# A hybrid encoder layer on one core: three of the seven staged SwiGLU combinations are split before they go to DRAM

## The chip, the cores and the metric

The kernel runs on one core of one Trainium2 chip, as one launch. The metric is the device time in microseconds, lower is better. The core has a matrix engine (TensorE, in the profile PE for its matmuls and PEld for its weight loads), a vector engine (VectorE, DVE), a scalar engine (ScalarE, ACT), GpSimd (POOL) and a queue engine that issues the DMAs (SyncE, SP). Matmuls accumulate in PSUM banks of 128 x 512 f32; all else lies in SBUF or in DRAM.

## The reference

One layer over 1024 tokens of width 1024: a SwiGLU half step, a combined mixer (HGRN2 heads and stick-breaking attention heads), a cross attention to 256 memory tokens, a second SwiGLU half step and a final norm. The change touches only the two SwiGLUs:

```python
D_FF = 2816

def swiglu(h, w_gu, w_down):
    gu = h @ w_gu
    gate, up = jnp.split(gu, 2, axis=-1)
    return (jax.nn.silu(gate) * up) @ w_down

x = x + 0.5 * swiglu(rmsnorm(x, ffn1_norm[l]), ffn1_w_gu[l], ffn1_w_down[l])
...
x = x + 0.5 * swiglu(rmsnorm(x, ffn2_norm[l]), ffn2_w_gu[l], ffn2_w_down[l])
```

The products are to have f32 accuracy. The kernel gets it by writing each factor as a high part (rounded to the matrix engine's fp32r) and a low part (the factor minus its high part), and by three matmuls for each pair of factors: high x high, high x low, low x high. Making a factor's two parts is called its split below: ACT copies the factor to the high part, DVE subtracts the high part from it.

## The kernel before

**Blocks and products.** All large products of a SwiGLU are done as jobs on 2 x 2 blocks in Winograd's form, with seven block products in place of eight. PRODUCTS (line 245) lists them: left factors A11, S1, S2, A12, S3, S4, A22 (weights or sums of weights), right factors B11, T1, T2, B21, T3, B22, T4 (activations or combinations of them), and the bank X, Y or Z that each adds to. One product is 12 matmuls of 128 x 512 (four row chunks of three matmuls each).

**Jobs.** The 2816 hidden columns are 22 chunks of 128, taken as 11 pairs p = 0 to 10. For each pair there is a gate job (gate_job) and an up job (up_job); pair 0 is done plainly ahead of the woven part. After the gate and the up job of a pair, four tiles a11, a12, a21, a22 of 128 x 512 hold its activations. store (line 792) forms from them T1 = a12 - a11, T2 = a22 - T1, T3 = a22 - a12, T4 = a21 - T2 with DVE, and SP writes seven tiles, B11 = a11, B21 = a21, B22 = a22 and T1 to T4, to DRAM (256 KB each). The second projection is made of down jobs (down_job, line 864): GROUPS (line 636) gathers the pairs as 0 to 3, 4 to 7 and 8 to 10, and each group has four down jobs, one for each quarter of the output columns. They are called group 0, 1 and 2 below. In the second SwiGLU the last group holds only pairs 8 and 9 (plain_last); pair 10 is multiplied plainly at the very end and stores only four tiles, a12 under the name T3. A product of group 2 thus has 9 matmuls in the first SwiGLU and 6 in the second.

**The return.** When group g starts, its seven combinations are fetched for its three or four pairs: fetches (line 822) loads each combination's tiles into the place of the low part (staged, line 806), seven products ahead of their first use; four products ahead ACT copies the high parts, three products ahead DVE subtracts in place. The split parts then serve all four jobs of the group. Names in the profile: T is a tile with both parts of a T1, T2 or T4; hh and hl are the high and the low part of B11, B21, B22 and T3; f is a split weight block, S a sum of weight blocks (made by POOL), r the raw weights, E and e are 128 x 512 activation or output tiles, sg a small pool of four such tiles, fa0B to fa10B and fa0T to fa10T (ga... in the second SwiGLU) the DRAM tiles.

**The order of the work.** Two streams of jobs (gate jobs and then down jobs with e = 0, 2; up jobs and then down jobs with e = 1, 3) are woven product by product, the second lagging by 3 products (weave, line 314; LAG, line 247). Each engine's recorded instructions keep the order in which the program emits them (in_order, line 71), so all of them carry line 83 in the profile. At each product i, weave.run issues the product's matmuls, the read of its bank (which frees the bank for the next product), the deferred steps that have come due (defer(n, step) runs a step n products later), and then prepares the products ahead by fixed leads (line 248):

```python
LOAD, SUM, FETCH, HI, LO, FETCHED_HI, FETCHED_LO = 7, 6, 7, 5, 4, 4, 3
```

So DVE's queue holds, in the order of the products: bank reads, low parts of weight blocks, the gating products, the combinations of store, and at a group's start the low parts of the fetched tiles, three or four at a time. There are two PSUM buffers for each of X, Y and Z. In group 1 of a SwiGLU the residual x, which has been put away in DRAM, is brought back through tiles of the sg pool (to_x, line 814). Pair 0's tiles are stored by a deferred step (line 984).

Of the kernel before, what the change touches and what calls it, by code (L numbers as in the profile page):

```python
# [8 lines left out]
F32 = mybir.dt.float32  # L9
# [9 lines left out]
P = 128  # L19
# [12 lines left out]
def hybrid_layer(ctx, tc, x, mem, ffn1_norm, ffn1_w_gu, ffn1_w_down, mix_norm, w_in, hg_lb_raw,  # L32
# [611 lines left out]
        return hp.tile([P, H], F32R, name=f"hh{c}_{hf}"), hp.tile([P, H], F32R, name=f"hl{c}_{hf}")  # L644

    NORMED = 8

    def swiglu(rs, ys, g0, w_gu, w_down, blk, first, tag, done, tail, head, stored=False, hook=None, side=None, plain_last=False, lift=None):
        with ExitStack() as st:
# [1 line left out]
            psx = pool(st, "psx", 1, PSUM, "right")  # L651
            B = {"B11": [hT[0][2 * j] for j in range(4)], "B21": [hT[0][2 * j + 1] for j in range(4)],
                 "B22": [hT[1][2 * j + 1] for j in range(4)], "T1": [], "T2": [], "T3": [], "T4": []}
            ad = [{k: dram.tile([P, H], F32, name=f"{tag}a{p}{k}") for k in B} for p in range(FP)]
            xd = {}
            pools = {}

            def E(brief=False):
                if brief or "ep" not in pools:
                    return pools["e0"].tile([P, H], F32, name="e")  # L660
                return pools["ep"].tile([P, H], F32, name="E")
# [115 lines left out]
            def up_job(p):  # L777
# [11 lines left out]

                return job(blk, w_gu, 0, 4, FF + 2 * p * P, B.get, summed(u[p], use))  # L790

            def store(p, a11, a12, a21, a22):
                if plain_last and p == FP - 1:
                    for k, t in (("B11", a11), ("B21", a21), ("B22", a22), ("T3", a12)):
                        nc.sync.dma_start(out=ad[p][k], in_=t)
                    return
                t1, t2, t3, t4 = (E(i < 2) for i in range(4))
                dve.tensor_tensor(t1, a12, a11, op=ALU.subtract)
                dve.tensor_tensor(t2, a22, t1, op=ALU.subtract)
                dve.tensor_tensor(t3, a22, a12, op=ALU.subtract)  # L800
                dve.tensor_tensor(t4, a21, t2, op=ALU.subtract)
                for k, t in (("B11", a11), ("T1", t1), ("B22", a22), ("T2", t2), ("T3", t3), ("B21", a21), ("T4", t4)):
                    nc.sync.dma_start(out=ad[p][k], in_=t)


            def staged(p, bk, n):
                hi, lo = slot(blk, bk, n)
                nc.sync.dma_start(out=lo.bitcast(F32), in_=ad[p][bk])
                return hi, lo

            acc = {}
# [10 lines left out]
            def fetches(p0, pn):  # L822
                Bg = {}

                def fetch(bk, what):
                    if what == 0 and bk not in Bg:
                        Bg[bk] = [staged(p0 + n, bk, n) for n in range(pn)]
                        stack[p0, bk] = 0
                    if what and stack[p0, bk] < what:
                        stack[p0, bk] = what  # L830
                        for hi, lo in Bg[bk]:
                            if what == 1:
                                act.activation(hi, lo.bitcast(F32), AF.Copy)
                            else:
                                dve.tensor_tensor(lo, lo.bitcast(F32), hi.bitcast(F32), op=ALU.subtract)

                return Bg.get, fetch
# [26 lines left out]
            def down_job(p0, pn, e, get, fetch):  # L864
                ends = (p0, pn) == last_group[0]

                def read(fk, bank):
# [6 lines left out]
                    if plain_last and ends:  # L874
                        if (e, fk) == (1, "A11"):
                            for half, ks in enumerate((("B11", "B21"), ("T3", "B22"))):
                                plains[half] = [staged(FP - 1, k, 3) for k in ks]
                            for n, t in enumerate(plains[0] + plains[1]):
                                pairs.defer(7 + n, lambda t=t: split_staged([t]))
                            pairs.defer(1, load_rows_last)  # L880
                        elif (e, fk) == (2, "A22"):
                            for n, (k, b) in enumerate(((0, 0), (0, 1), (1, 0), (1, 1))):
# [98 lines left out]
            pairs.defer(1, lambda: flow([sums_4(2), sums_4(3)], 2))  # L981
            pairs.defer(2, x_away)
            pairs.defer(4, open_mp)
            pairs.defer(14, lambda: store(0, s[0][0], s[1][0], s[0][1], s[1][1]))
            pairs.run()

            if plain_last:
# [719 lines left out]
```

## Time and profile before

| | |
|---|---|
| median of 3 runs | 2322.42 us (2320.59 to 2324.09) |
| the profiled execution | 2320.99 us |
| its span, from the first to the last instruction | 2319.3 us |
| mean granted clock of TensorE | 0.991 |
| bytes moved by DMA | 228.03 MB (HBM read 166.49, written 59.51) |

The gate and up jobs of the first SwiGLU lie between about 86 and 442 us of the span, those of the second between about 1705 and 2055 us; the down jobs follow each. The profile's page gives for each engine its busy time, its share of the span and its count of instructions. The view of windows gives the same for a stretch of time, with the granted clock of TensorE, the share in which the DMA engines were busy, and the GB/s they moved. The view of waits lists who was waited for: the waiting engine and its line, an arrow, the engine, tile and line that released it, then the total in us, the number of times and the longest. In a timeline a row is a start, a duration, the engine, the operation with output, inputs, shape and count, and in brackets the idle time of the engine before it and what ended that. Matmuls overlap: one lasts 0.39 us in such a row, though the next starts after 0.23 us.

### The profile page before, as it was taken

How to read it: one execution, taken by the hardware profiler on the slowest of the kernel's cores; microseconds unless marked ns; L12 is line 12 of the kernel's file. 1: busy time of each engine (PE TensorE's matmuls, PEld its weight loads, DVE VectorE, ACT ScalarE, POOL GpSimd, SP SyncE). 2: the span in 40 equal slices, each digit the busy share in tenths (PEclk: the TensorE clock that was granted, in tenths of full speed). 3: DMA queues.
4: the chain of work that ended last, by engine and by line, in shares of the span. 5: the costliest groups of instructions: out<-in, count | busy, mean ns of one | idle time of the engine just before them, and what ended most of it. 6: DMA issues, size and time to landing. Idle time of an engine off the chain costs nothing. (4 is left out here: it accounts for less than half of the span.)

```text
span 2319.3 us, 31224 instructions
## 1 busy us (share of the span) xinstructions
PE 2236.2 (96%) x11330; PEld 1869.4 (81%) x11330; DVE 1692.2 (73%) x2832; ACT 980.0 (42%) x1885; POOL 731.5 (32%) x686
## 2 busy tenths in 40 slices
PE   8899999999999999999999999999989999999988
PEld 7788888777778788888979888887778888878767
DVE  5866667869985878778697536567586666786997
ACT  6434333444354536344364333224443333344334
POOL 2343446434541102011032020001335343643543
PEclk9999999999999999999999999999999999999999
DMA  6243333545622000001005311111332323274441
GB/s 218 90 138 109 123 109 118 196 135 160 192 93 64 19 29 28 28 28 28 27 25 169 118 37 55 46 37 41 123 132 91 117 94 111 90 236 130 135 135 73
DMA packets 198665, 228.03 MB, mean 98 GB/s; under 512 B 10928, under 2 KB 140016, under 8 KB 198512
## 3 DMA queue, kind: packets, MB, share of 16 engines
q1 hardware_dynamic: 198512, 226.04, 30.2%
q8 instruction: 89, 1.46, 0.3%
q14 instruction: 64, 0.52, 0.1%
HBM read 166.49 MB, written 59.51 MB: 97 GB/s over the span
## 5 line engine op out<-in xcount | busy, mean ns | idle before, releaser
L83 PE MATMUL X<-T,f 128*128 128x512 f32 x1464 | 348.0, 393 | 14.7 <-ACT e L83 10.8
L83 PEld LDWEIGHTS X<-T,f 128*128 128x128 f32 x1464 | 276.7, 190 | 75.2 <-ACT e L83 11.7
L83 PE MATMUL X<-hh,f 128*128 128x512 f32 x975 | 316.1, 394 | 15.6 <-DVE E L83 14.1
L83 ACT ACTIVATE f<-S 128x512 fp32r<-128x512 f32 (+2 forms) x256 | 154.4, 608 | 347.0 <-POOL S L83 346.6
L83 DVE TENSOR_TENSOR f<-S,f 128x512 fp32r<-128x512 f32 (+2 forms) x256 | 255.3, 1005 | 27.4 <-ACT f L83 25.9
L83 PEld LDWEIGHTS X<-hh,f 128*128 128x128 f32 x975 | 185.2, 190 | 59.6 <-ACT f L83 9.2
L83 POOL TENSOR_TENSOR E<-E,rs 128x512 f32<-128x512 f32 x112 | 180.0, 1608 | 121.5 <-DVE E L83 104.3
L83 DVE TENSOR_TENSOR f<-r,f 128x512 fp32r<-128x512 f32 (+2 forms) x192 | 200.8, 1063 | 0.3
L83 POOL TENSOR_TENSOR S<-r,r 128x512 f32<-128x512 f32 (+2 forms) x64 | 97.0, 1515 | 316.1 <-DVE E L83 93.6
L83 PE MATMUL X<-hl,f 128*128 128x512 f32 x488 | 192.4, 394 | 2.8 <-DVE hl L83 2.8
L83 PE MATMUL Y<-T,f 128*128 128x512 f32 x732 | 177.0, 390 | 0.2 <-DVE T L83 0.2
L83 PEld LDWEIGHTS Y<-T,f 128*128 128x128 f32 x732 | 137.2, 188 | 29.6 <-DVE T L83 1.1
L83 PE MATMUL Z<-hh,f 128*128 128x512 f32 x488 | 160.7, 389 | 0.0
L83 PE MATMUL Y<-hh,f 128*128 128x512 f32 x488 | 160.7, 389 | 0.0
L137 PE MATMUL acc<-hh,wh 128*128 128x512 f32 (+1 forms) x384 | 153.1, 399 | 0.0
L83 POOL TENSOR_TENSOR S<-S,r 128x512 f32<-128x512 f32 (+2 forms) x64 | 82.3, 1286 | 211.6 <-DVE f L83 211.6
L138 PE MATMUL acc<-hl,wh 128*128 128x512 f32 (+1 forms) x384 | 145.1, 378 | 1.4 <-DMA hl<-msl 1.4
L139 PE MATMUL acc<-hh,wl 128*128 128x512 f32 (+1 forms) x384 | 145.3, 378 | 0.0
L83 ACT ACTIVATE E<-X 128x512 f32<-128x512 f32 x102 | 60.5, 594 | 192.8 <-PE X L83 192.8
L1140 POOL TENSOR_SCALAR_AFFINE_SELECT om<-om 128x128 f32<-128x128 f32 x64 | 27.2, 424 | 355.2 <-ACT om L1135 354.9
L83 DVE TENSOR_TENSOR E<-X,E 128x512 f32<-128x512 f32 x98 | 67.3, 686 | 84.3 <-PE X L83 84.1
L117 ACT ACTIVATE wh<-wraw 128x512 fp32r<-128x512 f32 (+1 forms) x128 | 79.0, 654 | 103.1 <-PE acc L138 41.6
(465 smaller groups left out, 5490.4 us busy)
## 6 DMA issues: line engine op xcount, KB each, us to landing
r<-in_ffn_w_gu_dram SPq DMA_DIRECT2D x86, 512.0 KB
r<-in_ffn_w_down_dram SPq DMA_DIRECT2D x32, 512.0 KB
wraw<-in_w_in_dram SPq DMA_DIRECT2D x20, 512.0 KB
wraw<-in_mem_w_kv_dram SPq DMA_DIRECT2D x16, 512.0 KB
T<-in_x_dram SPq DMA_DIRECT2D x8, 512.0 KB
fx<-x SPq DMA_DIRECT2D x16, 256.0 KB
sg<-fx SPq DMA_DIRECT2D x16, 256.0 KB
xs<-E SPq DMA_DIRECT2D x16, 256.0 KB
```

Source lines behind the costliest of these rows:

```text
L83: done = getattr(self.eng, name)(*args, **kw)
L117: nc.scalar.activation(hi[:, part], src[:, part], AF.Copy)
L137: nc.tensor.matmul(ps, lh, rh, start=start, stop=False)
L138: nc.tensor.matmul(ps, lh, rl, start=False, stop=False)
L139: last_mm[0] = nc.tensor.matmul(ps, ll, rh, start=False, stop=stop).ins
L1140: nc.gpsimd.affine_select(out=a[:, dg], in_=a[:, dg], compare_op=ALU.is_gt, fill=fill, base=0, pattern=[[-1, P]], channel_multiplier=1)
```

## The change

SPLIT names three combinations, T1, B21 and T4. When a pair is stored, these three are split first: ACT copies the high part into a tile of the sg pool (for pair 0 into one of the pools of e or E tiles) and SP stores it; one product later DVE subtracts the high part in place, and SP stores the low part. On return both parts are loaded, each by a DMA of its own, and the copy and the subtraction at lead 4 and 3 are left out for them. T2, B11, T3 and B22 are stored whole and split on return as before. Beside this, the seven tiles of a pair are stored in another order, pair 0 is stored one product earlier, and in the second SwiGLU the four tiles of pair 10 are stored one to four products after their turn, one at a time.

```diff
--- before.py
+++ after.py
@@ -644,6 +644,7 @@
         return hp.tile([P, H], F32R, name=f"hh{c}_{hf}"), hp.tile([P, H], F32R, name=f"hl{c}_{hf}")
 
     NORMED = 8
+    SPLIT = ("T1", "B21", "T4", )
 
     def swiglu(rs, ys, g0, w_gu, w_down, blk, first, tag, done, tail, head, stored=False, hook=None, side=None, plain_last=False, lift=None):
         with ExitStack() as st:
@@ -651,7 +652,7 @@
             psx = pool(st, "psx", 1, PSUM, "right")
             B = {"B11": [hT[0][2 * j] for j in range(4)], "B21": [hT[0][2 * j + 1] for j in range(4)],
                  "B22": [hT[1][2 * j + 1] for j in range(4)], "T1": [], "T2": [], "T3": [], "T4": []}
-            ad = [{k: dram.tile([P, H], F32, name=f"{tag}a{p}{k}") for k in B} for p in range(FP)]
+            ad = [{k: [dram.tile([P, H], F32, name=f"{tag}a{p}{k}{e}") for e in ("hl" if k in SPLIT else "a")] for k in B} for p in range(FP)]
             xd = {}
             pools = {}
 
@@ -789,23 +790,39 @@
 
                 return job(blk, w_gu, 0, 4, FF + 2 * p * P, B.get, summed(u[p], use))
 
+            def keep(p, k, t):
+
+                if k not in SPLIT:
+                    nc.sync.dma_start(out=ad[p][k][0], in_=t)
+                    return
+                hi = pools["sg"].tile([P, H], F32, name="sg") if p else E()
+                act.activation(hi.bitcast(F32R), t, AF.Copy)
+                nc.sync.dma_start(out=ad[p][k][0], in_=hi)
+
+                def low():
+                    dve.tensor_tensor(t.bitcast(F32R), t, hi, op=ALU.subtract)
+                    nc.sync.dma_start(out=ad[p][k][1], in_=t)
+
+                pairs.defer(1, low)
+
             def store(p, a11, a12, a21, a22):
                 if plain_last and p == FP - 1:
-                    for k, t in (("B11", a11), ("B21", a21), ("B22", a22), ("T3", a12)):
-                        nc.sync.dma_start(out=ad[p][k], in_=t)
+                    for n, (k, t) in enumerate((("B11", a11), ("B21", a21), ("B22", a22), ("T3", a12))):
+                        pairs.defer(1 + n, lambda k=k, t=t: keep(p, k, t))
                     return
                 t1, t2, t3, t4 = (E(i < 2) for i in range(4))
                 dve.tensor_tensor(t1, a12, a11, op=ALU.subtract)
                 dve.tensor_tensor(t2, a22, t1, op=ALU.subtract)
                 dve.tensor_tensor(t3, a22, a12, op=ALU.subtract)
                 dve.tensor_tensor(t4, a21, t2, op=ALU.subtract)
-                for k, t in (("B11", a11), ("T1", t1), ("B22", a22), ("T2", t2), ("T3", t3), ("B21", a21), ("T4", t4)):
-                    nc.sync.dma_start(out=ad[p][k], in_=t)
+                for n, (k, t) in enumerate((("T1", t1), ("T2", t2), ("B11", a11), ("B21", a21), ("T3", t3), ("B22", a22), ("T4", t4))):
+                    keep(p, k, t)
 
 
             def staged(p, bk, n):
                 hi, lo = slot(blk, bk, n)
-                nc.sync.dma_start(out=lo.bitcast(F32), in_=ad[p][bk])
+                for t, part in zip((hi, lo) if bk in SPLIT else (lo,), ad[p][bk]):
+                    nc.sync.dma_start(out=t.bitcast(F32), in_=part)
                 return hi, lo
 
             acc = {}
@@ -826,7 +843,7 @@
                     if what == 0 and bk not in Bg:
                         Bg[bk] = [staged(p0 + n, bk, n) for n in range(pn)]
                         stack[p0, bk] = 0
-                    if what and stack[p0, bk] < what:
+                    if what and stack[p0, bk] < what and bk not in SPLIT:
                         stack[p0, bk] = what
                         for hi, lo in Bg[bk]:
                             if what == 1:
@@ -875,8 +892,9 @@
                         if (e, fk) == (1, "A11"):
                             for half, ks in enumerate((("B11", "B21"), ("T3", "B22"))):
                                 plains[half] = [staged(FP - 1, k, 3) for k in ks]
-                            for n, t in enumerate(plains[0] + plains[1]):
-                                pairs.defer(7 + n, lambda t=t: split_staged([t]))
+                            for n, (k, t) in enumerate(zip(("B11", "B21", "T3", "B22"), plains[0] + plains[1])):
+                                if k not in SPLIT:
+                                    pairs.defer(7 + n, lambda t=t: split_staged([t]))
                             pairs.defer(1, load_rows_last)
                         elif (e, fk) == (2, "A22"):
                             for n, (k, b) in enumerate(((0, 0), (0, 1), (1, 0), (1, 1))):
@@ -981,7 +999,7 @@
             pairs.defer(1, lambda: flow([sums_4(2), sums_4(3)], 2))
             pairs.defer(2, x_away)
             pairs.defer(4, open_mp)
-            pairs.defer(14, lambda: store(0, s[0][0], s[1][0], s[0][1], s[1][1]))
+            pairs.defer(13, lambda: store(0, s[0][0], s[1][0], s[0][1], s[1][1]))
             pairs.run()
 
             if plain_last:
```

In groups 0 and 1 four low parts, one for each pair, leave DVE's queue at each of three places; each store gets three. The first place on DVE is the start of group 0 in the first SwiGLU. X and Z are PSUM banks, rs0 the row scale with which a gate result is read. Before, from the last two low parts of B11 (hl4_0 and hl6_0) on:

```order
L83 TENSOR_TENSOR hl4_0_3769<-hl4_0_3769,hh4_0_3768 128x512
L83 TENSOR_TENSOR hl6_0_3772<-hl6_0_3772,hh6_0_3771 128x512
L83 TENSOR_TENSOR E_3888<-X_3575,rs0_669 128x512
L83 TENSOR_TENSOR f_3861<-S_3837,f_3861 128x512
L83 TENSOR_TENSOR E_3751<-Z_3898,E_3751 128x512
L83 TENSOR_TENSOR E_3751<-E_3751,E_3588 128x512
L83 TENSOR_TENSOR f_3891<-S_3658,f_3891 128x512
L83 TENSOR_TENSOR T10_3811<-T10_3811 128x512
L83 TENSOR_TENSOR T11_3813<-T11_3813 128x512
L83 TENSOR_TENSOR T12_3815<-T12_3815 128x512
L83 TENSOR_TENSOR T13_3817<-T13_3817 128x512
```

With the change the last two low parts of B11 are followed by:

```order
L83 TENSOR_TENSOR hl4_0_3922<-hl4_0_3922,hh4_0_3921 128x512
L83 TENSOR_TENSOR hl6_0_3925<-hl6_0_3925,hh6_0_3924 128x512
L83 TENSOR_TENSOR E_4045<-X_3716,rs0_702 128x512
L83 TENSOR_TENSOR f_4018<-S_3994,f_4018 128x512
L83 TENSOR_TENSOR E_3904<-Z_4051,E_3904 128x512
L83 TENSOR_TENSOR E_3904<-E_3904,E_3729 128x512
L83 TENSOR_TENSOR f_4048<-S_3799,f_4048 128x512
L83 TENSOR_TENSOR f_4069<-S_3994,f_4069 128x512
L83 TENSOR_TENSOR E_3957<-X_3891,E_3957 128x512
L83 TENSOR_TENSOR E_3957<-E_3957,E_3776 128x512
```

and ahead of them stand, from the store of pair 9 (e, E and E with an sg tile):

```order
L83 TENSOR_TENSOR E_3729<-Z_3867,E_3729 128x512
L83 TENSOR_TENSOR e_3842<-e_3842,sg_3850 128x512
L83 TENSOR_TENSOR E_3832<-E_3832,sg_3855 128x512
L83 TENSOR_TENSOR E_3845<-E_3845,sg_3860 128x512
L83 TENSOR_TENSOR f_3864<-S_3650,f_3864 128x512
L83 TENSOR_TENSOR f_3889<-S_3799,f_3889 128x512
L83 TENSOR_TENSOR E_3776<-X_3716,E_3776 128x512
```

T10 to T13 are gone from behind the read of Z, as are the four of B21 (hl1_0 to hl7_0) and of T4 further on. New are the three rows with sg tiles, the low parts of T1, B21 and T4 of pair 9; they stand 13 to 15 rows ahead of the read E_4045<-X,rs0.

The second place on DVE is the start of group 2 in the first SwiGLU, where a combination has three tiles. Before, from the read of an X bank through the low parts of T1:

```order
L83 TENSOR_TENSOR f_5222<-S_5016,f_5222 128x512
L83 TENSOR_TENSOR T10_5145<-T10_5145 128x512
L83 TENSOR_TENSOR T11_5147<-T11_5147 128x512
L83 TENSOR_TENSOR T12_5149<-T12_5149 128x512
L83 SCALAR_TENSOR_TENSOR E_3947<-X_5260,E_3947 128x512
L83 SCALAR_TENSOR_TENSOR E_4552<-E_4552,sg_5217 128x512
L83 TENSOR_TENSOR f_5246<-S_5172,f_5246 128x384
L83 TENSOR_TENSOR E_4473<-X_5077,E_4473 128x512
L83 SCALAR_TENSOR_TENSOR E_4423<-E_4423,sg_5242 128x512
L83 TENSOR_TENSOR f_5277<-r1_4956,f_5277 128x512
L83 TENSOR_TENSOR T20_5198<-T20_5198 128x512
L83 TENSOR_TENSOR T21_5200<-T21_5200 128x512
```

and now:

```order
L83 TENSOR_TENSOR f_5366<-S_5157,f_5366 128x512
L83 SCALAR_TENSOR_TENSOR E_4100<-X_5401,E_4100 128x512
L83 SCALAR_TENSOR_TENSOR E_4709<-E_4709,sg_5361 128x512
L83 TENSOR_TENSOR f_5387<-S_5316,f_5387 128x384
L83 TENSOR_TENSOR E_4626<-X_5218,E_4626 128x512
L83 SCALAR_TENSOR_TENSOR E_4576<-E_4576,sg_5383 128x512
L83 TENSOR_TENSOR f_5418<-r1_5097,f_5418 128x512
L83 TENSOR_TENSOR T20_5342<-T20_5342 128x512
L83 TENSOR_TENSOR T21_5344<-T21_5344 128x512
L83 TENSOR_TENSOR T22_5346<-T22_5346 128x512
```

The three T1 rows between the weight block f and the read of X are gone; the T2 rows stand as they did.

The third place is SP's queue where group 0's loads begin in the first SwiGLU, behind the stores of pair 9. Before:

```order
L803 DMA fa9T1_616<-e_3701 128x512
L803 DMA fa9T2_617<-e_3702 128x512
L803 DMA fa9T3_618<-E_3703 128x512
L803 DMA fa9T4_619<-E_3704 128x512
L808 DMA hl0_0_3763<-fa0B11_550 128x512
L808 DMA hl2_0_3766<-fa1B11_557 128x512
L808 DMA hl4_0_3769<-fa2B11_564 128x512
L808 DMA hl6_0_3772<-fa3B11_571 128x512
L808 DMA T10_3811<-fa0T1_553 128x512
```

and now:

```order
L800 DMA fa9T4h_648<-sg_3860 128x512
L804 DMA fa9T1l_645<-e_3842 128x512
L804 DMA fa9B21l_642<-E_3832 128x512
L804 DMA fa9T4l_649<-E_3845 128x512
L825 DMA hl0_0_3916<-fa0B11a_550 128x512
L413 DMA r1_3913<-in_ffn1_w_down_dram 128x4x256
L825 DMA hl2_0_3919<-fa1B11a_560 128x512
L825 DMA hl4_0_3922<-fa2B11a_570 128x512
L825 DMA hl6_0_3925<-fa3B11a_580 128x512
L825 DMA T10_3964<-fa0T1h_554 128x512
L825 DMA T10_3964<-fa0T1l_555 128x512
```

The loads now stand behind three stores of low parts (names ending in l), which DVE's subtractions have to release, and each T1 tile has two loads, of its high and of its low part.

## The prediction

> **What bounds the kernel now.** I read the page's first part, then the two gate/up stretches and the six stalled stretches as windows. Columns: stretch, its length, then busy time and instruction count of PE, PEld, DVE, ACT and POOL, granted clock, DMA share, GB/s.
>
> ```profile
> PE 2236.2 (96%) x11330; PEld 1869.4 (81%) x11330; DVE 1692.2 (73%) x2832; ACT 980.0 (42%) x1885; POOL 731.5 (32%) x686
> 86.00:442.00 356.00, 356.00 (x1579) 294.70 (x1579) 246.36 (x324) 138.74 (x255) 169.61 (x115) 1.00 0.39 125
> 1705.00:2055.00 350.00, 350.00 (x1546) 289.82 (x1545) 235.64 (x270) 126.40 (x226) 166.77 (x113) 1.00 0.36 117
> ```
>
> PE has 96% of the span, and in the 706 us of gate and up jobs it never pauses while DVE is busy 69% (246.36 of 356.00; 235.64 of 350.00). There a lighter DVE brings nothing, and added DVE work is free as long as it fits. What can be won lies where PE stops, in the down jobs. I call the starts of down groups 0, 1 and 2 A, B and C, with a 1 or 2 for the SwiGLU.
>
> ```profile
> 441.49:481.56 40.07, 35.65 (x145) 27.77 (x144) 39.93 (x48) 24.88 (x47) 16.67 (x11) 0.96 0.68 231
> 560.44:576.06 15.62, 14.05 (x62) 11.10 (x60) 15.62 (x19) 3.42 (x6) 11.36 (x8) 1.00 0.39 116
> 605.98:652.03 46.05, 40.50 (x158) 30.70 (x157) 46.05 (x60) 19.30 (x38) 21.27 (x16) 0.93 0.50 164
> 2055.88:2090.02 34.14, 30.89 (x133) 24.46 (x132) 34.04 (x40) 21.44 (x41) 16.17 (x10) 1.00 0.67 230
> 2171.62:2187.23 15.61, 14.06 (x62) 11.10 (x60) 15.61 (x19) 3.42 (x6) 11.34 (x8) 1.00 0.36 118
> 2217.15:2255.76 38.61, 32.65 (x133) 23.99 (x132) 38.24 (x58) 14.39 (x34) 18.07 (x15) 1.00 0.37 116
> 2047.88 5.44 PE Y L83 x24
> ```
>
> The last row, of the chain of waits, gives the step of a matmul at full speed: 5.44/24 = 0.2267 us. The stretches hold 144, 60, 156, 132, 60 and 132 matmuls of whole products (the counts in the rows take in neighbours at the edges). Length minus matmuls times the step is what PE loses: **A1** 40.07-32.64 = 7.4, **B1** 2.0, **C1** 46.05-35.37 = 10.7, **A2** 4.2, **B2** 2.0, **C2** 8.7: 35.0 us, the ceiling of any gain. DVE is busy 98 to 100% in all six. Who holds PE there, from the waits of 440 to 660 and of 2050 to 2275 (total, times, longest):
>
> ```profile
> PE X L83 <- DVE E L83: 6.4, 4, 2.5
> PE X L83 <- DVE T L83: 2.1, 1, 2.1
> PE X L83 <- DVE hl L83: 1.9, 3, 0.7
> PE X L83 <- DVE E L83: 7.7, 6, 1.8
> PE X L83 <- DVE T L83: 1.8, 1, 1.8
> ```
>
> All is DVE: a factor's low part that is late (T, hl), or the read of an X bank (E) that stands behind a burst of low parts in DVE's queue. X is wanted again first, as the next product for it comes soonest.
>
> **The change part by part.** The counts of copies and subtractions stay the same. Of each product pair, three of the seven splits move from the group's start to the store: one ACT copy and one DVE subtraction each. Of a group of four pairs that takes 12 subtractions out of the start, of C1 9. Each split tile costs one store and one load of 256 KB more.
>
> C, where the most is lost. DVE's timeline (start, duration) in C1, with a wait of PE at 631.70, then DVE in C2:
>
> ```profile
> 612.45 2.99 DVE L83 TENSOR_TENSOR T<-T 128x512 fp32r<-128x512 f32 x3
> 624.80 4.62 DVE L83 TENSOR_TENSOR hl<-hl,hh 128x512 fp32r<-128x512 f32 x3
> 639.79 1.88 DVE L83 TENSOR_TENSOR hl<-hl,hh 128x512 fp32r<-128x512 f32 x3
> 643.73 1.88 DVE L83 TENSOR_TENSOR T<-T 128x512 fp32r<-128x512 f32 x3
> 631.70 0.76 PE L83 MATMUL X<-hh,f 128*128 128x512 f32 x1 [1.49 <-DVE E L83]
> 2222.31 2.39 DVE L83 TENSOR_TENSOR T<-T 128x512 fp32r<-128x512 f32 x2
> 2232.93 2.92 DVE L83 TENSOR_TENSOR hl<-hl,hh 128x512 fp32r<-128x512 f32 x2
> 2246.96 1.28 DVE L83 TENSOR_TENSOR T<-T 128x512 fp32r<-128x512 f32 x2
> ```
>
> T1 (612.45), B21 (624.80) and T4 (643.73) go: 2.99+4.62+1.88 = 9.5 us. B22 (639.79) stays. The same subtraction takes 0.63 in the rows of 1.88 and 1.54 in that of 4.62. Undisturbed the step is 0.60 (2.49 for four in A1 below: the first 0.68, then 0.60 each), so 9 are worth at least 5.4. If what stretched them (POOL, busy 21.27 of the 46.05) stretches the next subtraction instead, only the 5.4 are saved. DVE is full, so PE follows it one to one up to its loss of 10.7. I take the middle of 5.4 and 9.5: **C1 -7.4**. In C2 six such (2.39+2.92+1.28 = 6.6) and the plainly multiplied pair's B21 (0.6, by the same step) go: 7.2 at most, 7 x 0.6 = 4.2 at least: **C2 -5.8**, the middle rounded up.
>
> The Trainium skill, "SBUF — State Buffer", section "Who interferes with whom", says that a DVE instruction with two SBUF inputs contends with a GpSimd instruction that reads SBUF; the spread from 0.63 to 1.54 agrees. By that rule the POOL operation finds the next two-input subtraction and C falls to its lower ends, 5.4+4.2, which would make the sum 3.6 less; the rows alone as they stand would make it 16.7.
>
> B. The last burst of group 1 is T4:
>
> ```profile
> 562.67 2.49 DVE L83 TENSOR_TENSOR T<-T 128x512 fp32r<-128x512 f32 x4
> ```
>
> With the 2.49 gone from inside the stretch, and eight more ahead of it, DVE is ahead by more than the 2.0 that PE loses: **B1 -2.0, B2 -2.0** (bounds 0 and 2.0).
>
> A. Two stalls. DVE and PE in A1:
>
> ```profile
> 441.41 1.10 DVE L83 TENSOR_TENSOR f<-S,f 128x512 fp32r<-128x512 f32 x1 [1.75 <-ACT f L83]
> 444.14 4.67 DVE L83 TENSOR_TENSOR hl<-hl,hh 128x512 fp32r<-128x512 f32 x4
> 448.73 0.68 DVE L83 TENSOR_TENSOR E<-X,rs 128x512 f32<-128x512 f32 x1
> 453.52 3.59 DVE L83 TENSOR_TENSOR T<-T 128x512 fp32r<-128x512 f32 x4
> 463.90 2.49 DVE L83 TENSOR_TENSOR hl<-hl,hh 128x512 fp32r<-128x512 f32 x4
> 449.56 0.47 PE L83 MATMUL X<-hh,f 128*128 128x512 f32 x1 [2.46 <-DVE E L83]
> 450.22 1.05 PE L83 MATMUL X<-hh,f 128*128 128x512 f32 x2
> 477.57 0.50 PE L83 MATMUL X<-hl,f 128*128 128x512 f32 x1 [0.73 <-DVE hl L83]
> 2063.23 0.47 PE L83 MATMUL X<-hh,f 128*128 128x512 f32 x1 [1.75 <-DVE E L83]
> 2084.23 0.47 PE L83 MATMUL X<-hh,f 128*128 128x512 f32 x1 [1.50 <-DVE E L83]
> ```
>
> The first stall stays: B11 (444.14) is not among the split ones, and it holds the read at 448.73. After the gap of 2.46 matmuls come 0.43 apart (two in 1.05 at 450.22) until about 453; with clock 0.96 over 40.07 that is 1.6 us. The three low parts of the pair before the last now stand ahead of this burst (rows in the part on the change). They are 3 x 0.6 = 1.8 us; the idle 1.75 ahead of 441.41 can take some of it, but it ends by an ACT copy whose input comes by way of POOL and DVE. I charge 1.0 of growth (bounds 0 and 1.8), and in A1 0.6 for a longer slow stretch. A1's second loss (the three waits ending with 477.57, with their matmuls 2.8) goes: T1 (3.59) and B21 (2.49) are out of DVE ahead of it, 6.1 us, against 1.8 for the last pair's low parts. **A1** -2.8+1.0+0.6 = **-1.2** (-3 to +1). In A2 the second stall (1.50, 1.7 with its slow first matmul) goes the same way, the first grows by 1.0 to 2.75 and may then be followed by half speed, as the 2.46 were: half of 1.6, 0.8. **A2** -1.7+1.0+0.8, about **0** (-1.7 to +2). The Trainium skill, "TensorE: Matmul & The Clock Gate", puts the fall to half speed at an idle window of about 3.4 us; by it A2's 0.8 would drop out, but the 2.46 in A1 were enough.
>
> The gate/up stretch. Each store adds three ACT copies and three low parts, one product after the store. Windows of one product each at a store, in the second SwiGLU:
>
> ```profile
> 1966.12:1968.84 2.72, 2.72 (x14) 2.25 (x13) 2.72 (x5) 0.02 (x1) 1.34 (x2) 1.00 0.92 347
> 1968.84:1971.56 2.72, 2.72 (x14) 2.25 (x13) 2.05 (x2) 2.14 (x4) 1.98 (x2) 1.00 0.02 6
> 1974.28:1976.99 2.71, 2.71 (x13) 2.25 (x12) 0.50 (x1) 1.64 (x3) 1.32 (x2) 1.00 0.60 189
> ```
>
> DVE is full in the store's product, has 0.7 free in the next and 2.2 free two later. Three low parts (1.8, 2 with a POOL overlap) push the bank read by up to 1.3 us and are caught up at the third; a read is late for PE only after a whole product of 2.72. ACT's copies (0.61 each, about 1.8) fill its near idle product (0.02 busy). So 0; if that cover were gone, 20 stores at up to 1 us. The moved orders of stores and x loads and the first store one product earlier fall into the same idle DMA and cost 0.
>
> DMA. In group 0 twelve loads and, with the last pairs', about three stores more, 15 x 0.262 = 3.9 MB:
>
> ```profile
> 455.00:468.00 13.00, 13.00 (x59) 10.77 (x58) 12.93 (x20) 7.63 (x15) 2.11 (x2) 1.00 0.90 310
> 2041.00:2064.00 23.00, 21.25 (x95) 17.30 (x93) 18.66 (x21) 11.31 (x22) 14.87 (x11) 1.00 0.94 307
> 2069.00:2083.00 14.00, 13.74 (x60) 10.99 (x59) 13.93 (x21) 7.03 (x14) 3.50 (x2) 1.00 0.97 343
> ```
>
> At 307 to 343 GB/s that is 11 to 13 us of transfer. A1 and A2 leave 40.07 x 0.32 = 12.8 and 34.14 x 0.33 = 11.3 us of idle transfer time, and loads are issued seven products ahead, 19 us; a tile that comes back split is wanted only at its product, an unsplit one four products earlier by ACT. I take 0; B and C have shares of 0.36 to 0.50 and room.
>
> Sum: -1.2+0-2.0-2.0-7.4-5.8 = **-18.4**. The span of the profiled execution goes from 2319.3 to 2300.9, its time from 2320.99 to 2302.6. The median of the runs, 2322.42, lies 1.4 above that execution: **2304**.
>
> **The rivals.** (1) *All bursts dissolve.* DVE gets so far ahead in B and C that the T2, T3 and B22 splits are early too: C1 and C2 gain their whole 10.7 and 8.7, B 4.0, A its second stalls (2.8+1.7): 27.9, so 2294.5. For it: DVE alone is named in the waits. Against: in C, DVE had no idle time in 46.05 us, and 9 subtractions less do not make the rest shorter. (2) *The burst is only displaced.* C gains the lower ends less what B22 and T3 still hold, say half of 9.6, B half of 4.0, and each A loses the upper 1 and 2 us: -4.8-2+3 = -3.8, about 2318.5. For it: what holds C1 at 631.70 is a read behind a burst, and four bursts of seven remain. Against: B and C have 40 subtractions fewer, all ahead of a waiting PE. (3) *Transfers become the bound at A: slower.* At shares of 0.90 to 0.97 the 11 to 13 us do not find the idle time, since SP issues in order and a low part's store waits for DVE with the loads of group 0 behind it. Then A1 and A2 each lose 12 and B and C win 17.2: +6.8, 2329. It decides from an exposure of 17.2/2 = 8.6 us at each A, so nearly all of the added transfer. (4) *It does nothing of the kind*: the copies hold ACT's queue in order, waiting for the fourth combination, and each of 20 stores costs 1 us: 2304+20 = 2324.
>
> **How the numbers follow.** Forecast 0.55, (1) 0.12, (2) 0.20, (3) 0.07, (4) 0.06. The forecast's own terms run from A +3, B 0, C -9.6 (together -6.6) to A -4.7, B -4, C -16.7 (-25.4); as they will not all meet one end, its own range is -11 to -23: 2299 to 2311. For 8 in 10 the range takes in (1) on one side and most of (2) on the other: **2294 to 2319**. A measurement of this kernel can tell 0.2%, 4.6 us, from no change: faster is under 2317.8. That is the forecast, (1) and about half of (2): 0.55+0.12+0.11 = 0.78, with two of a hundred more for a forecast whose C is small falling on this side: 0.80. Same holds the rest of (2) and part of (4): 0.11; slower (3) and the bad end of (4): 0.09.
>
> **What would show it.** In the profile after, A1's first stall should still stand as a wait of 2.5 us or more for DVE E, at the first read after B11; A1's waits for hl near its end, B's whole loss and A2's wait of 1.50 should be gone. C1 should lose 2 to 5 us instead of 10.7 and C2 2 to 4 instead of 8.7. DVE's busy time at the three group starts falls, its sum over the span stays within some 10 us of 1692.2 (what POOL stretches), the gate/up stretches stay at PE 100%, and bytes rise by about 130 x 0.262 = 34 MB from 228. Waits of PE, ACT or DVE for a DMA in A show rival (3); PE below 100% in the gate/up stretches, behind ACT, shows (4). I am wrong in the main if C loses over 8 us still.

## The result and the profile after

The change makes the kernel faster: 2312.19 us (2308.91 to 2314.56, 4 runs) against 2321.97 of the kernel before beside it (2320.59 to 2324.09, 4 runs). The ratio is 0.9947, with a 95% interval of 0.9932 to 0.9961, that is 9 to 16 us. The two medians differ by 9.8 us, the ratio gives 12. The forecast was 2304, 18 us less. The measured time lies in the stated range (2294 to 2319), but just above the forecast's own range of 2299 to 2311. The direction is as predicted, and so are B and most of C, but not A; the size is half to two thirds of the forecast.

The first part of the page of the profiled execution (2312.28 us, span 2310.6):

```profile
PE 2235.9 (97%) x11330; PEld 1872.0 (81%) x11330; DVE 1687.0 (73%) x2832; ACT 988.1 (43%) x1885; POOL 731.5 (32%) x686
```

The windows of the two gate/up stretches and of the six stretches of the prediction, cut at the starts of products, with the prediction's columns:

```profile
86.50:442.50 356.00, 356.00 (x1578) 294.66 (x1579) 267.44 (x354) 156.36 (x282) 169.81 (x113) 1.00 0.42 140
1702.00:2052.00 350.00, 350.00 (x1546) 289.82 (x1545) 256.35 (x301) 145.95 (x254) 168.31 (x112) 1.00 0.39 132
442.19:486.76 44.57, 39.20 (x158) 31.02 (x156) 38.86 (x46) 21.84 (x40) 18.37 (x12) 0.92 0.86 314
562.92:576.52 13.60, 13.60 (x62) 11.26 (x60) 11.52 (x13) 4.10 (x7) 9.69 (x7) 1.00 0.29 95
606.44:658.86 52.42, 49.99 (x211) 38.63 (x210) 50.41 (x65) 21.70 (x43) 29.88 (x22) 1.00 0.64 212
2053.66:2088.52 34.86, 31.77 (x134) 25.86 (x132) 31.58 (x34) 19.96 (x37) 16.85 (x11) 0.95 0.87 316
2170.12:2183.72 13.60, 13.60 (x62) 11.26 (x60) 11.54 (x13) 4.10 (x7) 9.70 (x7) 1.00 0.32 97
2213.64:2252.66 39.02, 36.97 (x157) 28.73 (x156) 38.32 (x62) 12.36 (x30) 19.00 (x17) 1.00 0.47 156
```

The gate/up stretches took in 21 us of DVE work each (246.36 to 267.44, 235.64 to 256.35) and PE still never pauses. B1 and B2 last 13.60 us, exactly their 60 matmuls: nothing is lost. C1's window holds 210 matmuls (4 products of 12, 18 of 9), 47.6 us, so it loses 4.8; C2's holds 156, 35.4 us, and loses 3.7. A1, however, takes 44.57 us for 156 matmuls (35.37) and loses **9.2, more than the 7.4 before**, at a clock of 0.92; A2 takes 34.86 for 132 (29.92) and loses 4.9 in place of 4.2.

All losses below are worked out in this way, product by product: the time from the start of one product to that of the next, minus its 12, 9 or 6 matmuls by 0.2267 us. In the table A is counted over its first 16 products (192 matmuls), and C runs on to the end of group 2, which adds 0.8 to C2 of before. With all seven split 2.1 us more of A1's loss fall behind that cut. Kernels are compared with runs of the kernel before on the same chip.

| kernel | median us | ratio (95%) | A1 | B1 | C1 | A2 | B2 | C2 |
|---|---|---|---|---|---|---|---|---|
| before | 2322.42 | | 7.4 | 2.0 | 10.7 | 4.2 | 2.0 | 9.5 |
| before again | 2324.41 | 1.0004 (0.9993 to 1.0014) | 7.5 | 2.0 | 10.8 | 4.2 | 2.0 | 9.4 |
| **the change** | 2312.19 | 0.9947 (0.9932 to 0.9961) | 9.2 | 0 | 4.9 | 4.9 | 0 | 3.8 |
| the change again | 2311.79 | 0.9952 (0.9937 to 0.9967) | 7.8 | 0 | 4.9 | 4.9 | 0 | 3.7 |
| order alone | 2324.42 | 1.0005 (0.9995 to 1.0014) | 7.4 | 1.3 | 10.8 | 4.3 | 1.4 | 9.4 |
| transfers alone | 2321.68 | 0.9989 (0.9980 to 0.9999) | 7.5 | 0.7 | 10.8 | 4.0 | 2.0 | 9.5 |
| low parts 5 and 8 later | 2312.92 | 0.9951 (0.9936 to 0.9966) | 8.2 | 0 | 4.4 | 5.2 | 0 | 3.7 |
| low parts 10 and 12 later | 2307.05 | 0.9937 (0.9918 to 0.9955) | 5.3 | 0 | 4.9 | 2.0 | 0 | 3.9 |
| without T4 | 2308.68 | 0.9931 (0.9914 to 0.9948) | 6.6 | 0.1 | 5.0 | 4.2 | 0.1 | 5.3 |
| with B11 | 2302.65 | 0.9908 (0.9892 to 0.9925) | 6.4 | 0 | 3.0 | 1.1 | 0 | 3.5 |
| with B11, low parts later | 2297.88 | 0.9888 (0.9873 to 0.9903) | 2.4 | 0 | 3.0 | 0 | 0 | 3.5 |
| the same, loads 5 ahead | 2306.84 | 0.9930 (0.9914 to 0.9947) | 6.5 | 0 | 3.5 | 4.4 | 0 | 3.5 |
| **T3 in place of T4** | 2295.47 | 0.9878 (0.9864 to 0.9893) | 0.4 | 0.1 | 1.8 | 0.3 | 0.1 | 3.4 |
| all seven | 2329.51 | 1.0025 (1.0014 to 1.0035) | 16.4 | 0 | 0.1 | 7.3 | 0 | 2.1 |

The losses of before and of the change repeat within 0.2 us in a second execution, apart from A1's 9.2 and 7.8. There only the length of the half-speed stretch differs (3.0 and 1.5 us): these are the matmuls after a stall that start 0.43 us apart in place of 0.23.

In the change the six stretches together lose 22.9 us, before 35.8: 13.0 less, or 14.5 with the second execution of the change. That agrees with both ratios. The two profiled executions differ by only 8.7 in span; the rest lies outside the stretches. Its main part is one wait, in the cross attention (before, then the change, from PE's timeline):

```profile
1233.86 0.39 PE L138 MATMUL acc<-hl,wh 128*128 128x256 f32 x1 [1.36 <-DMA hl<-msl]
```

```profile
1229.61 0.58 PE L138 MATMUL acc<-hl,wh 128*128 128x256 f32 x1 [2.52 <-DMA hl<-msl]
```

The wait for one transfer is 1.2 us longer, and the matmuls after it come at a slower rate for a while; together that is 2.6 us of the 4.3.

### The profile page after: what moved, and what is told of

It is laid out like the page before. It is cut to its first block, busy times and chain, and to the rows that moved or that the text cites. A ratio compares the mean times of both kernels' runs of the same rounds, so it can differ in the third digit from the quotient of the medians.

```text
span 2310.6 us, 31427 instructions
## 1 busy us (share of the span) xinstructions
PE 2235.9 (97%) x11330; PEld 1872.0 (81%) x11330; DVE 1687.0 (73%) x2832; ACT 988.1 (43%) x1885; POOL 731.5 (32%) x686
## 5 line engine op out<-in xcount | busy, mean ns | idle before, releaser
L83 DVE TENSOR_TENSOR f<-S,f 128x512 fp32r<-128x512 f32 (+2 forms) x256 | 233.0, 923 | 38.6 <-ACT f L83 37.9
```

The lines of the kernel that those rows point to most:

```text
L83: done = getattr(self.eng, name)(*args, **kw)
```

## The experiments

**Is the rest chance?** Both kernels were run a second time as they are.

> The changed kernel once more, for what differs outside the two SwiGLUs. Theory (that is chance of a single execution: a wait for a DMA in the cross attention and the half-speed stretch behind it): the six stretches repeat within 0.3 us each, the part between the two SwiGLUs is anywhere from 995 to 1003 us, and the median is 2309 to 2313. Rival (the change itself makes that part slower): it is 1000 us or more again.

> The kernel before once more, for the same question. Theory (chance): the stretches repeat within 0.3 us, and the part between the two SwiGLUs is anywhere from 995 to 1003 us. Rival (the change makes that part slower): it is at 997 again, within 1 us.

The stretches repeat, apart from A1 of the change (table). From the end of the first SwiGLU's products to the start of the second's the two executions of before took 997.4 and 999.2 us, those of the change 1000.5 and 1002.0; over all fourteen profiles it is 995.7 to 1005.0. The wait for that transfer was 2.68 us in before's second execution, longer than in the change's first. So the wait varies by itself from one execution to the next. But the theory is not clear of doubt: 1002.0 fits the rival as well, and the five profiles that split T1 and B21 and not B11 have 1000.1 to 1005.0, the nine others 995.7 to 999.6. That wait alone is not the reason, as in one of the five (without T4, below) it is only 0.69 us. Whether the change adds some 2 us there stays open; no run tells it apart.

**Is the new order free?** All of the change but the split:

```diff
-    SPLIT = ("T1", "B21", "T4", )
+    SPLIT = ()
```

> All of the change but its split: no combination is split at the store, all seven return whole and are split on return; the new order of the stores, the first store one product earlier and the later x loads stay. Theory (the gain is DVE's shorter bursts, the reordering is free): the six stretches lose what they lose before, A1 7.4, B1 2.0, C1 10.7, A2 4.2, B2 2.0, C2 8.7, and the time is 2322 (2319 to 2325). Rival (the 4 us that the two profiled executions differ by outside the six stretches belong to the reordering): 2325 to 2327 with the same losses in the stretches.

The ratio is 1.0005 and A and C are as before; B came out 0.7 and 0.6 better, which was not expected and is too small to see in the time. The order of the stores, the earlier first store and the later x loads are worth nothing measurable.

**What do the transfers cost?** The same, but T1, B21 and T4 are stored and loaded twice:

```diff
+    TWICE = ("T1", "B21", "T4", )
...
+                    if k in TWICE:
+                        pairs.defer(1, lambda: nc.sync.dma_start(out=ad[p][k][1], in_=t))
...
-                for t, part in zip((hi, lo) if bk in SPLIT else (lo,), ad[p][bk]):
+                for t, part in zip((hi, lo) if bk in TWICE else (lo,), ad[p][bk][::-1]):
```

> Like the kernel without any split at the store, but T1, B21 and T4 are stored twice and loaded twice (the second copy into the place of the high part, where ACT's copy then overwrites it): the transfers of the change without its split. Theory (the transfers hide): within 2 us of the kernel that only reorders, A1 and A2 as there. Rival (transfers in A cost): A1 grows from 7.4 to 9 or more and A2 from 4.2 to 5 or more, with waits of ACT for a DMA, and the time is 3 us or more above the kernel that only reorders. Here ACT needs both loads four products ahead, so this is the dearer side of the change's own transfers.

A1 is 7.5 and A2 4.0, and the kernel is no slower than with the order alone. Both this kernel and the change move 33.6 MB more than the kernel before. The added bytes hide, as predicted; rival (3) falls for this change. One of its signs does show in the change: POOL waits 9.8 us for down weights in A1 and ACT 4.7 us just behind it, where before neither waited. But PE waits for no DMA there, and two runs have such waits without the added loss: this one (11.6 and 2.3) and, below, the low parts ten products later (10.6 and 3.4).

**Why did A grow?** DVE in A1 of the change, then the wait of PE:

```profile
431.43 1.47 DVE L83 TENSOR_TENSOR e<-e,sg 128x512 fp32r<-128x512 f32 x1
432.82 2.38 DVE L83 TENSOR_TENSOR E<-E,sg 128x512 fp32r<-128x512 f32 x2
437.44 0.68 DVE L83 TENSOR_TENSOR E<-X,E 128x512 f32<-128x512 f32 x1
443.86 1.10 DVE L83 TENSOR_TENSOR f<-S,f 128x512 fp32r<-128x512 f32 x1 [2.84 <-ACT f L83]
446.59 4.63 DVE L83 TENSOR_TENSOR hl<-hl,hh 128x512 fp32r<-128x512 f32 x4
451.15 0.68 DVE L83 TENSOR_TENSOR E<-X,rs 128x512 f32<-128x512 f32 x1
451.97 0.77 PE L83 MATMUL X<-hh,f 128*128 128x512 f32 x1 [4.18 <-DVE E L83]
```

The three rows with sg are the low parts of pair 9: 431.43 to 435.13, 3.7 us and not the 1.8 of three undisturbed ones. Behind them the read at 437.44 is late (at 434.14 before, in an execution that ran 0.7 ahead, so by 2.6). And still DVE idles for 2.84 us just after, ahead of 443.86: it waits for ACT's copy of a sum that POOL makes, and POOL's queue was late, as it had waited for DVE's read. So the idle time that I had counted on as a cushion is itself an effect of the delay. PE waits 4.18 us in place of 2.46. The first test put pair 9's low parts five products later, into that idle time, and those of pair 10 eight:

```diff
-                pairs.defer(1, low)
+                pairs.defer(n, low)
...
-                    keep(p, k, t)
+                    keep(p, k, t, {FP - 2: 5, FP - 1: 8}.get(p, 1))
```

> The change, with the low parts of the last two pairs computed and stored later: those of pair 9 five products after the store in place of one, those of pair 10 eight. Theory (A grew because three low parts of pair 9, 3.7 us with POOL beside them, delay the reads ahead of group 0, and those of pair 10 hold the T3 and B22 bursts): A1 falls from the change's 9.2 to about 4.3 and A2 from 4.9 to about 2.0, the rest as in the change; 2304 to 2306. Rival (A grew by transfers or by ACT's copies): A1 and A2 stay at 9 and 5, 2311 to 2313.

It failed: the first stall of A1 is 4.0 us, that of A2 3.6. DVE there:

```profile
440.74 1.38 DVE L83 TENSOR_TENSOR e<-e,sg 128x512 fp32r<-128x512 f32 x1
442.04 3.49 DVE L83 TENSOR_TENSOR E<-E,sg 128x512 fp32r<-128x512 f32 x2
445.45 1.78 DVE L83 TENSOR_TENSOR f<-S,f 128x512 fp32r<-128x512 f32 x1
```

The idle time is gone, since the chain by way of POOL is now in time. In its place the low parts take 4.7 us (440.74 to 445.45) directly ahead of the weights' low part and the B11 burst. By either way the read came about as late. That fits the low parts as the cause, but it fits the rival (ACT's copies) as well, so they were put behind the read altogether:

```diff
+                    keep(p, k, t, {FP - 2: 10, FP - 1: 12}.get(p, 1))
```

> The change, with the low parts of pair 9 ten products after the store (behind the first read of group 0 in DVE's queue) and those of pair 10 twelve. Theory (A's first stall grew because pair 9's three low parts, with POOL beside them 3.7 to 4.8 us of DVE, stand ahead of that read, whether early or just ahead of it): the first stall of A1 falls from 4.3 to 2.6 and its slow stretch from 3.0 to 1.7, in A2 from 3.3 to 1.9 and from 1.7 to 0.1; A1 5 to 6, A2 2 to 3 in all, 2306 to 2309. Rival (ACT's three copies at the store hold the sums of POOL behind them, and that is what delays the read): first stalls stay at about 4 and 3.3, 2311 to 2314.

```profile
448.87 0.68 DVE L83 TENSOR_TENSOR E<-X,rs 128x512 f32<-128x512 f32 x1
458.39 0.69 DVE L83 TENSOR_TENSOR e<-e,sg 128x512 fp32r<-128x512 f32 x1
449.69 0.47 PE L83 MATMUL X<-hh,f 128*128 128x512 f32 x1 [2.17 <-DVE E L83]
```

The wait is 2.17, near the 2.46 of before, A1 5.3 and A2 2.0, and the time 2307.05 us, 4.7 below the change on the same chip. The intervals of the two ratios overlap there; the stretches, which lose 5.4 to 6.8 less, agree with the gain. ACT's copies stayed where they were, so the rival falls. A's growth is the place of pair 9's low parts (first stall), and the half-speed stretch that follows a longer gap. A1's end gains too (1.2 in place of 1.9): there pair 10's low parts had stood between the bursts of T3 and B22.

**Which split brings what?** First T4 alone was put back:

```diff
-    SPLIT = ("T1", "B21", "T4", )
+    SPLIT = ("T1", "B21", )
```

> The change with only T1 and B21 split at the store; T4 is stored whole and split on return as before. Step B of the prediction (B's loss goes since T4's burst of 2.49 us is out of that stretch): B1 and B2 lose 2.0 each again, 2314 to 2317. Theory after the run with T3 in place of T4 (it is the eight subtractions of T1 and B21 ahead of the stretch that let DVE arrive early, and T4's own burst then no longer holds PE): B1 and B2 stay under 0.3; C1 loses 5 to 6 and C2 4 to 5, as T4 is the last burst of a group; A1 and A2 lose half to 1 less than in the change, with two low parts of pair 9 in place of three; 2309 to 2313.

B1 and B2 lose 0.1 though T4's burst is in place, and longer than before:

```profile
559.22 3.58 DVE L83 TENSOR_TENSOR T<-T 128x512 fp32r<-128x512 f32 x4
```

So B's gain is from T1's and B21's eight subtractions earlier in the group. C1 is 5.0 without T4's split and 4.9 with it, C2 5.3 and 3.8; in A the third low part costs 1.2 to 2.7 and 0.8, of which 0.6 in each first stall. Over all, T4's split gains nothing that shows: 2308.68 us without it, 2312.19 and 2311.79 with it, on different chips.

**With B11 split as well,** the burst that holds A's first read should go:

```diff
-    SPLIT = ("T1", "B21", "T4", )
+    SPLIT = ("B11", "T1", "B21", "T4", )
```

> The change with B11 split at the store as well, four of seven. Theory (A's first stall is B11's burst of four low parts, 4.6 us, ahead of the read of the first bank): the first stall of A1 falls from 4.3 and its slow stretch of 2.9 to about 1 together, that of A2 from 3.3 and 1.7 to about 0.5, C gains 1 to 2; 2300 to 2304. Rival (a fourth low part of pair 9 ahead of the same read costs what the burst gives back): A1 and A2 within 1 of the change's 9.2 and 4.9, 2309 to 2313. Rival (transfers bind at A): A1 above 10 with waits for a DMA.

Both first stalls and both half-speed stretches are gone (0 us). A2 is 1.1. A1 still loses 6.4, all near its end, where pair 10 now has four low parts between T3 and B22. The gate and up jobs of the first SwiGLU lose 1.1 us more than before, the first sign that low parts do not fit everywhere. Time 2302.65, as expected. With the low parts of pairs 9 and 10 later by ten and twelve products:

> B11, T1, B21 and T4 split at the store, and the low parts of pairs 9 and 10 computed ten and twelve products later. Theory (both findings add up: B11's burst is gone from the first stall, and no pair's low parts stand ahead of a read or of the T3 burst at group 0's start): A1 falls from 6.4 with B11 alone to 2.5 to 3.5, A2 from 1.1 to 0.5 to 1, the rest as with B11 alone; 2297 to 2300. Rival (what A1 still loses there is weights that come late behind the added loads): A1 stays at 5 to 7, 2301 to 2304.

A1 falls to 2.4, A2 to 0, the time to 2297.88. ACT still waits 9.9 us in two for the down weights in this stretch; PE's own waits there are 1.2 us for hl on DVE and 0.5 us for E on ACT. To see whether the weights should go first all the same, the split tiles were loaded five products ahead in place of seven:

```diff
-            for what, lead in ((2, FETCHED_LO), (1, FETCHED_HI), (0, FETCH)):
+            for what, lead in ((2, FETCHED_LO), (1, FETCHED_HI), (3, 5), (0, FETCH)):
...
-                    if what == 0 and bk not in Bg:
+                    if what == (3 if bk in SPLIT else 0) and bk not in Bg:
```

> The same, and the tiles that come back split are loaded five products ahead of their use in place of seven, behind the weights that are needed first. Theory (ACT's waits for the down weights at group 0, 12.9 us in two with B11 split, come from the split tiles' loads queued ahead): these waits shrink by half or more, and A1 falls by up to 1 more if they still decide; 2296 to 2300. Rival (five products are too few): PE waits for a DMA of T, hh or hl by 1 us or more at group 0.

The waits of ACT for weights fell to 0.5 us, and it got 9 us slower. PE now waits for the tiles themselves (430 to 520, and the first of 2040 to 2130):

```profile
PE X L83 <- DMA T<-fa0T4h: 1.3, 1, 1.3
PE X L83 <- DMA T<-fa0T4l: 0.7, 1, 0.7
PE X L83 <- DMA T<-ga2T4h: 1.7, 1, 1.7
```

The rival held: five products are too few. With the half-speed stretch behind these waits A1 loses 4.1 and A2 4.4 us more. The stall at the end of A1 (1.8 us) is no shorter (2.0) with ACT's waits gone, so those waits were not what held PE there. Transfers are close to binding in A with four splits: between 440 and 500 the DMA engines are busy for 0.90 of the time in the run with B11. Last, T3 in place of T4, with the later low parts:

> B11, T1, B21 and T3 split at the store (T3 in place of T4), with the later low parts. Theory (each stall belongs to the burst just ahead of it: T4's to B, T3's to the X stall near the end of A1 and in the middle of C): B1 and B2 lose about 2.0 each again, C1 falls from 3.0 to 1 to 1.5, C2 from 3.5 to 2, A1 to 1 to 2; 2297 to 2300. Rival (what counts is only how many subtractions are left, not which): B stays at 0 and C1 and C2 at 3.0 and 3.5.

2295.47 us, below the range expected and the fastest of all, 28 us under the kernel before. A1 0.4, A2 0.3, C1 1.8: T3's burst was the one that held PE in A's end and in much of C1. C2 stays at 3.4 (3.5 with T4), against the 2 expected. B stays at 0.1, so a stall does not belong to the burst just ahead of it alone, as the theory had it, but to all that DVE still owes from earlier bursts. All that PE waits for between 430 and 660 (total, times, longest):

```profile
PE X L83 <- DVE E L83: 1.2, 1, 1.2
PE X L83 <- ACT E L83: 0.3, 1, 0.3
```

**All seven split:**

```diff
-    SPLIT = ("T1", "B21", "T4", )
+    SPLIT = ("B11", "B21", "B22", "T1", "T2", "T3", "T4", )
```

> All seven combinations split at the store. Theory (a burst not moved is a stall kept): C1 and C2 fall from 4.9 and 3.8 to 1 and 1, B stays 0; the gate and up jobs stay without loss, since DVE has 0.7 to 2.2 us free in each product; A1 and A2 5 and 2; 2298 to 2304. Rival (transfers bind: 28 loads more for group 0 than before): A1 and A2 at 10 and 8 or more with waits for a DMA of the weights, 2310 or more. Rival (seven low parts per pair do not fit the gate and up jobs): those jobs lose 0.5 us or more at each store, 10 us in all.

Slower than before, 1.0025. C1 is 0.1 and C2 2.1, so the theory of the bursts holds to the end, but both rivals came true beside it (A2's 7.3 stays just short of the 8 named). The windows of the first gate and up jobs and of A1:

```profile
90.00:440.00 350.00, 344.86 (x1518) 282.43 (x1517) 275.54 (x378) 168.10 (x308) 160.50 (x107) 1.00 0.47 162
440.00:520.00 80.00, 66.26 (x268) 51.92 (x267) 49.65 (x57) 28.07 (x50) 32.06 (x21) 0.94 0.89 327
```

A wait of PE in the first window, and one of ACT in the second:

```profile
PE Y L83 <- DVE f L83: 4.3, 6, 1.1
ACT f L83 <- DMA r<-in_ffn_w_down_dram: 23.6, 2, 13.4
```

In the gate and up jobs PE loses 9.2 us more than before in the first SwiGLU and 4.9 in the second, though DVE is busy for only 79%: it waits for weight blocks' low parts on DVE, behind seven low parts in a row. In A DVE is idle for 38% of the time, because weights come up to 13.4 us late. In A the bound has moved from DVE to the transfers. All seven with the later low parts of the last two pairs was not run.

## Why the prediction was right or wrong, by its steps

**What bounds the kernel:** right. DVE's bursts at the group starts are the loss, the gate and up jobs had room for the moved work, and neither order nor transfers show in the time with three splits.

**B, -2.0 each:** right in size. The reason was half right: I named T4's 2.49 from inside the stretch and the eight subtractions ahead of it; without T4's split B is at 0.1 all the same. It is the eight.

**C1, -7.4:** measured -5.8 (10.7 to 4.9). The term of T4 is what was mis-sized. From the read at 608 to the one behind the B22 burst DVE's chain shortened by 5.3. Before:

```profile
608.04 0.68 DVE L83 TENSOR_TENSOR E<-X,E 128x512 f32<-128x512 f32 x1
630.41 0.54 DVE L83 TENSOR_TENSOR f<-r,f 128x384 fp32r<-128x384 f32 x1
641.60 0.68 DVE L83 SCALAR_TENSOR_TENSOR E<-X,E 128x512 f32<-128x512 f32 x1
```

With the change:

```profile
608.50 0.68 DVE L83 TENSOR_TENSOR E<-X,E 128x512 f32<-128x512 f32 x1
624.45 1.37 DVE L83 TENSOR_TENSOR f<-r,f 128x384 fp32r<-128x384 f32 x1
628.74 3.52 DVE L83 TENSOR_TENSOR hl<-hl,hh 128x512 fp32r<-128x512 f32 x3
636.72 0.68 DVE L83 SCALAR_TENSOR_TENSOR E<-X,E 128x512 f32<-128x512 f32 x1
```

33.56 became 28.22, with T1 (2.99) and B21 (4.62) gone: 5.3 of 7.6, between the 3.6 of six undisturbed subtractions and the whole, near the middle that I took. Most of the rest moved to neighbours: the same weight block's low part takes 1.37 where it took 0.54 (630.41 before, 624.45 now). That agrees in kind with the rule of the Trainium skill ("SBUF — State Buffer", "Who interferes with whom") that the prediction cites, but C1 did not fall to the lower end that the prediction tied to it. T4's 1.9, however, brought nothing in C1 (5.0 without it), since PE lost only 1.1 there and other reads were late in their turn. "PE follows it one to one up to its loss" was wrong behind the last burst. The half-speed stretch of C1 also went, its clock is 1.00 from 0.93; what that alone was worth is doubtful, as the last section shows.

**C2, -5.8:** measured -5.7 (9.5 to 3.8), of which T4 has 1.5.

**A1, -1.2, and A2, 0:** this step failed, by up to 3.0 and by 0.7. Measured are +1.8 (+0.3 in the second execution) and +0.7. Three terms of it were wrong: the first stall grew by 1.7 and 1.3, where I charged 1.0, because the three low parts cost 3.7 with POOL beside them and the idle time ahead of the burst was no cushion; the half-speed stretch grew by 1.2 in A1 (in the second execution it was 0.2 shorter than before's 1.7) and by 1.6 in A2 against 0.6 and 0.8; and A1's second loss, said to go whole (2.8), went only from 3.1 to 1.9, for pair 10's low parts came to stand beside the bursts that remained. The bound of +1 for A1 was too tight, since it took 1.8 as the most that three low parts can cost. The row with 4.62 for three of them was quoted in the same text.

In A2 PE's gap was 3.09 us and a half-speed stretch of 1.7 followed it, and one of 1.7 follows the gap of 2.17 in the run with the low parts ten products later. The idle window of about 3.4 us in the Trainium skill's page "TensorE: Matmul & The Clock Gate" (section "What's actually happening") would have left A2 at full speed. The measurement decides against the page's figure here.

**Transfers 0, gate and up jobs 0:** right for three splits, shown by the runs with the transfers alone and with the change. They are right up to a point only: with seven splits both fail, A in the way of rival (3), though PE is held there by ACT and DVE that wait for weights.

**The sum:** -18.4 forecast. The stretches gave -13.0: A missed by 3.7, C by 1.7. The profiled execution is 9.7 above the 2302.6 that was forecast for it; 5.4 are these, and the other 4.3 lie outside the stretches, where executions of one kernel differ too. Rival (2), a burst only displaced, holds for A: a displaced 3.7 us came back as a longer stall, and the +2.5 of the two A is near the +3 that it gave them. So the gain came as forecast in B and C, and the forecast failed in A.

## What to carry to other kernels

Moving work out of a burst into a stretch with idle time pays as long as the last moved pieces do not arrive just ahead of the next burst: look at the end of the donor stretch first, and place those pieces behind the first read that another engine waits for. Ask which burst holds the waiting engine, not how many can be moved: four well chosen splits with the last two pairs' low parts moved later gave 28 us, three gave 12 (18 with those low parts later), and seven, without that move, lost about 5. Idle time that ends by a chain through another engine can be the effect of one's own delay, and then it is no room.

## What was not expected of the hardware

A subtraction in a row of three on DVE that takes 0.6 us alone took 1.2 to 1.6 a tile (3.70 for three in the change, 4.71 for three with the low parts five products later) with POOL running beside it. The trace of the kernel before shows it throughout: of DVE's 128 x 512 subtractions with both inputs in SBUF, the 332 with no POOL instruction beside them took 0.59 to 0.69 us each, the 119 with POOL beside them all the time 1.69 in the median. Reads of a PSUM bank took at most 0.69 either way. The half-speed stretch after a gap is not of a fixed length: after the same first stall in A1 (4.34 and 4.33 us) it cost 3.0 us in one execution and 1.5 in the other. In the second execution of the kernel before no such stretch followed the gap (2.44) that in the first (2.46) had cost 1.7 (its loss there is 0.1). The window of its A1, as long as the first execution's 40.07 but at a clock of 1.00 in place of 0.96, and a wait 21 us on that the first execution did not have:

```profile
442.52:482.65 40.13, 34.27 (x146) 26.56 (x144) 39.99 (x48) 24.91 (x47) 16.48 (x11) 1.00 0.66 230
471.60 0.47 PE L83 MATMUL X<-hh,f 128*128 128x512 f32 x1 [1.52 <-DVE E L83]
```

So in the kernel before the half-speed stretch cost nothing in sum: DVE was full, and a faster PE only waited for it later. C1 shows the same, 10.7 and 10.8 us of loss at clocks of 0.93 and 0.96. In A1 of the change, where DVE has idle time, the 1.5 us between the two executions did come through. A slow stretch is to be priced only where the other engine has room, and the prediction's terms for it did not ask that.
